# A hybrid transformer trunk: the steps behind each output block are spread over the following blocks

## The chip, the cores and the metric

The kernel runs on one core of a Trainium2 chip. The metric is device time in microseconds, the median of the runs of a kernel; lower is better. The engines are TensorE (PE, with its weight loads shown as PEld), VectorE (DVE), ScalarE (ACT), GpSimd (POOL) and SyncE (SP, whose queue issues nearly all loads). Each takes its own instructions in order and waits for the others by semaphores.

## The reference

The input x is 512 tokens of width 1024 in float32; 16 learned meta tokens are put in front, so 528 rows run through two layers. Each layer adds three things to the running x:

```python
for i in range(DEPTH):
    h = h + 0.5 * swiglu(rmsnorm(h, ffn1_norm[i]), ffn1_w_in[i], ffn1_w_out[i])
    hn = rmsnorm(h, mix_norm[i])
    h = h + (diff_attention(hn, ...) if i % 2 == 0 else gla_mixer(hn, ...))
    h = h + 0.5 * swiglu(rmsnorm(h, ffn2_norm[i]), ffn2_w_in[i], ffn2_w_out[i])
return rmsnorm(h, final_norm)[:, N_META:]
```

SwiGLU is silu(g) * u with [g, u] = h @ w_in (1024 to 2 x 2816), times w_out (2816 to 1024). Attention has 8 heads, each with two softmax maps that are subtracted; GLA (gated linear attention) has 4 heads and goes chunk by chunk.

## The kernel before, in words

Everything is kept transposed: x is eight blocks `xr[0..7]` of 128 features by 528 tokens. The stages run in this order: SwiGLU a, attention (da), SwiGLU b, SwiGLU c, GLA, SwiGLU d. The order of each engine's instructions is written out by hand, so the order of calls in Python is the order of each queue.

Precision: a float32 factor is split in a high part (ACT copies it in a rounded type, fp32r) and a low part (DVE subtracts the high part from it), and a product is three matmuls: high x high, high x low, low x high. Weights come by DMA into the float32 tile `fa` and their parts go into the fp32r tile `ra`.

The input product of a SwiGLU is done by Strassen's scheme on 2 x 2 blocks. For a pair of x blocks (2i, 2i+1) and the two halves of the tokens, x has four quarters: the first (block 2i, first half, `plain` with k = 0, L403), the second and third (block 2i+1, both halves, k = 1), and the fourth (block 2i, second half, `plain2`, L670). Four sums of quarters follow: t1 (L422), t2, t3, t4 (L442, L445, L449), made from `scaled` copies (L415); ACT copies all four (L432), DVE makes their low parts (L435). With the three quarters these are the seven factors kept in `ra` (`seven`); the fourth quarter is kept in the last two hidden slots of the stage, so it is made only at the stage's beginning. It is used by the first hidden blocks alone, which are done plainly (products S1, S3, S2, S4; three blocks in stage a, one in b, c, d); from then on the products are P1, P2, P6, P7, P5, P3, P4. S products hold all four `bank` buffers of PSUM (S1 and S2 share two, S3 and S4 two); P1 of the next block needs one that DVE has read out (L710, or L712 where the root mean square isn't there yet).

The mean square is taken beside all this: `add_square` squares a block on ACT and POOL adds it to `acc` (L343); after the S3 of a stage (in a: after the S4 of block 1) `rms_scale` sums over partitions on PE (L383) and DVE refines the inverse root (L348 to L355).

The weight stream of a SwiGLU (`in_stream`) is a list of tasks: `cut` makes a weight's parts (ACT L597, DVE L622), `add` makes a Strassen sum of weights (DVE L611). After each product so many tasks are done that the parts of six products ahead are ready. After the hidden blocks of the last slab, the stage has a **tail**: eight output blocks j of 24 matmuls. DVE adds the accumulator to `xr[j]` (`out_done`, L849; in attention and GLA `project_out`, L501), which frees one of two accumulators, and then `next_block` makes what the next stage needs of that block:

```python
if kind == "seven":
    plain(i, gcol, tok, k)
add_square(acc, j, c0)
if kind == "seven":
    scaled(i, gcol, tok, k, z)
    if k:
        sums(i, tok, z, last and j == KD - 1)
```

All of a block's steps stand in the queues one behind the other, before the next block's addition. Between them the tail prepares the next stage's first weights (`nxt.to`, `ahead.to`). For stage a there is no tail ahead: `head` makes the quarters from x as it arrives and squares all blocks, and `head_sums` lists twelve steps for the sums, two of which are done behind each of the first products, after the stream's tasks. Until they are through, the stream makes no weight sums (`held`) and the first output weights aren't loaded (`bring`).

In attention, `k_done` (L1078) puts a head's keys in two maps `km` (L1087), in two buffers for alternating heads, which `score` reads (L1137, L1140).

## Time and profile before

| | |
|---|---|
| runs | 2125.42, 2125.94, 2127.83 us; median 2125.94 |
| the profiled execution's own time | 2127.64 us |
| its span, first to last instruction | 2125.9 us |
| busy | PE 1999.4 us (94%), DVE 1677.5 (79%), ACT 1026.2 (48%), POOL 260.5 (12%) |
| mean granted PE clock | 0.967 of 2.4 GHz |
| stages, P1 of b, c, d | at 772.83, 1156.46, 1769.83 us |

The profile is one execution. An engine's busy time is the union of its instructions; idle time is put down to what ended it. The granted clock has two levels, 1.2 and 2.4 GHz (0.5 and 1.0); a value between is a mean over a stretch. Neighbouring instructions of DVE or ACT overlap by about 0.1 us in these rows, so the step from one start to the next is a little shorter than the duration shown.

### The profile page before, as it was taken

The numbers are of one execution on the slowest core, as the hardware profiler recorded it, in microseconds if no ns is written. First come the engines' busy times: TensorE is split into PE (matmuls) and PEld (weight loads), VectorE is DVE, ScalarE is ACT, GpSimd is POOL, SyncE is SP. The second block draws the span as 40 slices with busy tenths as digits, with TensorE's granted clock in tenths as the row PEclk, the third lists the DMA queues.
The fourth block names the chain that finished last, engine by engine and source line by source line (L and its number), as shares of the span: only waits on it lengthen the run. The fifth ranks groups of instructions, "written<-read, shape, count | busy, mean of one in ns | idle before, by whom it ended". The sixth has DMA issues, their size and how long they took to land.

```text
span 2125.9 us, 36706 instructions
## 1 busy us (share of the span) xinstructions
PE 1999.4 (94%) x14672; PEld 1885.6 (89%) x14672; DVE 1677.5 (79%) x3104; ACT 1026.2 (48%) x2055; POOL 260.5 (12%) x193
## 2 busy tenths in 40 slices
PE   6999999999999979999997999999999989999997
PEld 5999999877777879999997999999888868999995
DVE  5888887678887789888867988887565678988884
ACT  6444444445555554444445444444645455544443
POOL 1000000534341200000001000000533310000002
PEclk8999999999998989999998999999999999999998
DMA  4233333111110223333321332332122122333331
GB/s 146 80 105 99 96 100 105 51 50 41 40 49 32 70 75 107 98 104 93 108 75 56 105 102 93 105 100 90 51 70 80 60 89 82 108 99 105 105 100 40
DMA packets 66285, 178.73 MB, mean 84 GB/s; under 512 B 7345, under 2 KB 13618, under 8 KB 66114
## 3 DMA queue, kind: packets, MB, share of 16 engines
q1 hardware_dynamic: 65792, 176.25, 26.6%
q8 instruction: 115, 1.88, 0.3%
q14 instruction: 56, 0.46, 0.1%
q10 hardware_dynamic: 322, 0.13, 0.0%
HBM read 174.26 MB, written 2.10 MB: 83 GB/s over the span
## 4 chain that ended last, share of the span: by engine, by line
PE 72%; DVE 18%; ACT 6%; issue 3%; POOL 1%; DMA 0%; SPq 0%; DVEq 0%; ACTq 0%; POOLq 0%
PE ps_ao L833 6%; PE ps_co L833 6%; PE ps_aA L782 5%; PE ps_cA L782 5%; PE ps_bA L782 5%; PE ps_bo L833 5%; PE ps_do L833 5%; PE ps_dA L782 4%; PE ps_bD L782 3%; PE ps_cD L782 3%; PE ps_aD L782 3%; PE ps_dak L269 2%; DVE ra L622 2%; PE ps_dD L782 2%; PE ps_aB L782 1%
## 5 line engine op out<-in xcount | busy, mean ns | idle before, releaser
L597 ACT CAST ra<-fa 128x512 fp32r<-128x512 f32 x630 | 376.6, 618 | 163.5 <-DVE fa L611 162.7
L622 DVE TENSOR_TENSOR ra<-fa,ra 128x512 fp32r<-128x512 f32 x630 | 426.9, 687 | 14.5 <-ACT ra L597 8.8
L611 DVE TENSOR_TENSOR fa<-fa 128x512 f32<-128x512 f32 x328 | 219.7, 686 | 2.9
L810 DVE TENSOR_TENSOR ra<-fa,ra 128x512 fp32r<-128x512 f32 (+1 forms) x160 | 101.4, 636 | 67.7 <-ACT ra L809 66.9
L225 POOL TENSOR_TENSOR ra<-fa,ra 128x1024 fp32r<-128x1024 f32 x51 | 122.7, 2408 | 158.1 <-ACT ra L222 130.7
L782 PE MATMUL ps_cA<-ra 128*128 128x264 f32 x1008 | 133.5, 284 | 1.8 <-ACT ftc L730 1.2
L782 PE MATMUL ps_bA<-ra 128*128 128x264 f32 x1008 | 133.5, 284 | 1.6 <-ACT ftb L730 1.0
L782 PE MATMUL ps_dA<-ra 128*128 128x256 f32 x1008 | 130.5, 281 | 2.6 <-ACT ftd L730 1.5
L782 PEld LDWEIGHTS ps_dA<-ra 128*128 128x128 f32 x1008 | 126.2, 188 | 7.1 <-ACT ftd L730 2.9
L782 PEld LDWEIGHTS ps_cA<-ra 128*128 128x128 f32 x1008 | 126.7, 188 | 2.8 <-ACT ftc L730 1.6
L782 PEld LDWEIGHTS ps_bA<-ra 128*128 128x128 f32 x1008 | 126.7, 188 | 2.6 <-ACT ftb L730 1.4
L782 PE MATMUL ps_aA<-ra 128*128 128x264 f32 x912 | 122.1, 286 | 3.6 <-DVE fta L710 3.2
L782 PEld LDWEIGHTS ps_aA<-ra 128*128 128x128 f32 x912 | 115.8, 190 | 4.4 <-issue 3.4
L809 ACT CAST ra<-fa 128x512 fp32r<-128x512 f32 (+1 forms) x160 | 91.5, 574 | 0.0
L833 PE MATMUL ps_bo<-hidb,ra 128*128 128x264 f32 x624 | 87.7, 290 | 0.0
L833 PE MATMUL ps_ao<-hida,ra 128*128 128x264 f32 x624 | 84.5, 283 | 0.0
L833 PE MATMUL ps_co<-hidc,ra 128*128 128x264 f32 x624 | 84.5, 283 | 0.0
L833 PEld LDWEIGHTS ps_bo<-hidb,ra 128*128 128x128 f32 x624 | 82.3, 195 | 0.0
L833 PE MATMUL ps_do<-hidd,ra 128*128 128x512 f32 x303 | 79.3, 394 | 0.0
L833 PEld LDWEIGHTS ps_ao<-hida,ra 128*128 128x128 f32 x624 | 79.3, 188 | 0.0
L833 PEld LDWEIGHTS ps_co<-hidc,ra 128*128 128x128 f32 x624 | 79.3, 188 | 0.0
L222 ACT CAST ra<-fa 128x1024 fp32r<-128x1024 f32 x64 | 66.8, 1046 | 5.5 <-issue 2.8
(546 smaller groups left out, 4377.5 us busy)
## 6 DMA issues: line engine op xcount, KB each, us to landing
fa<-in_f_in SPq DMA_DIRECT2D x174, 512.0 KB, 3.6
fa<-in_f_out SPq DMA_DIRECT2D x160, 256.0 KB, 2.7
fa<-in_da_in SPq DMA_DIRECT2D x24, 512.0 KB, 3.5
fa<-in_gla_in SPq DMA_DIRECT2D x24, 512.0 KB, 3.6
fa<-in_f_out SPq DMA_DIRECT2D x32, 128.0 KB, 2.1
fa<-in_da_out SPq DMA_DIRECT2D x8, 512.0 KB, 3.4
fa<-in_gla_out SPq DMA_DIRECT2D x8, 512.0 KB, 3.4
xr<-in_xT SPq DMA_DIRECT2D x8, 264.0 KB, 5.3
```

Source lines behind the costliest of these rows:

```text
L222: act.copy(h, w)
L225: eng.tensor_tensor(out=l, in0=w, in1=h.bitcast(F32), op=ALU.subtract)
L269: nc.tensor.matmul(put(b, at, at + c1 - c0), w[:, ws], x[:, c0:c1], start=first, stop=last,)
L597: act.copy(self.parts(n)[0], self.source(i))
L611: dve.tensor_tensor(out=self.raw(f, x), in0=self.raw(f, a), in1=self.raw(f, b), op=ALU.add)
L622: dve.tensor_tensor(out=l, in0=self.source(i), in1=h.bitcast(F32), op=ALU.subtract)
L782: nc.tensor.matmul(banks[k, f], w[:, ws], v, start=(p in ("P1", "P2", "P7") and i == 0 and c == 0), stop=(i == NQ - 1 and c == 2), skip_gr ...
L809: act.copy(h, raw)
L810: dve.tensor_tensor(out=l, in0=raw, in1=h.bitcast(F32), op=ALU.subtract)
L833: nc.tensor.matmul(ps[:, b, : a1 - a0], w[:, ws], x[:, a0:a1], start=(f == f0 and i == 0), stop=(f == f1 - 1 and i == 2),)
```

## The change

- `next_block` becomes a generator with up to four steps: (1) on ACT: the high parts of the block's quarters, the square, the scaled copy; (2) on DVE: the low parts of the quarters and the block's share of the four sums; for odd blocks also (3) on ACT the copy of the four sums and (4) on DVE their low parts. `follow`, called after a block's addition, takes each waiting generator one step on, does step 1 of the new block, and takes the older ones another step on. `drain` behind the last block finishes the rest. The special finer order for the last block is dropped.
- The fourth quarter is made with the first, for even blocks, in the tail. It lies in a room X2 at the end of `ra` that is shared: hidden slots 6 and 7, the fourth quarters, attention's two pairs of key maps, GLA's q parts and the meta keys' parts use it in turn. The scaled copies of odd pairs' even blocks get a room of their own (`other`).
- The parts of x for attention and GLA (`parts`) are stepped in the same way: the low part comes a block later.
- At the start of a: no squares in `head`; `head_later(u)` is called right behind each of the first nine products, before the stream's tasks, and does two squares (u < 4), the scaled copies of a pair (even u), or its sums and their copy (odd u), and the sums' low part one product later. `held` ends with the ninth product.

```diff
-RA = OB + 2 * L * KD
+X2 = OB + 2 * L * KD
+RA = X2 + NQ * 2 * HALF
...
-NHA = (RA - HB) // (2 * L)
+NHA = (X2 - HB) // (2 * L)
...
+    def second(i):
+        return parts_at(X2 + i * 2 * HALF, HALF)
+    def plain(i, gcol, tok, quarters):
...
+        todo = []
+        for q in quarters:
+            j = 2 * i + (q != 0 and q != 3)
+            x = tokens(xr[j], tok)
+            hl = seven(i)
+            if q == 0:
+                h, l, x = hl[0][:, 0, :n], hl[1][:, 0, :n], x[:, 0]
+            elif q == 1:
+                h, l = hl[0][:, 1:3, :n], hl[1][:, 1:3, :n]
+            else:
+                (h, l), x = [t[:, :n] for t in second(i)], x[:, 1]
+            g = vec[:, gcol + j : gcol + j + 1]
+            act.activation(h, x, AF.Copy, scale=g)
+            todo.append((l, x, g, h))
+        def rest():
+            for l, x, g, h in todo:
+                dve.scalar_tensor_tensor(l, x, g, h.bitcast(F32), op0=ALU.mult, op1=ALU.subtract)
+        return rest
...
-            z[:, 2 * k : 2 * k + 2, :n], tokens(xr[j], tok), AF.Copy,
+            z[k][:, :, :n], tokens(xr[j], tok), AF.Copy,
...
+    def sums(i, tok, z, k):
+        n = SEQ // 2 if tok else HALF
+        (b11, b12), (b21, b22) = [[t[:, c, :n] for c in range(2)] for t in z[:2]]
+        t1, t3, t2, t4 = [z[2][:, c, :n] for c in range(4)]
         if k == 0:
...
+            dve.tensor_tensor(out=t1, in0=b11, in1=b12, op=ALU.subtract)
+            return
+        dve.scalar_tensor_tensor(t2, b22, -1.0, t1, op0=ALU.mult, op1=ALU.subtract)
+        dve.tensor_tensor(out=t3, in0=b22, in1=b12, op=ALU.subtract)
+        dve.scalar_tensor_tensor(t4, t2, -1.0, b21, op0=ALU.mult, op1=ALU.subtract)
+    def cut_sums(i, tok, z, part):
+        n = SEQ // 2 if tok else HALF
+        h, l = [t[:, 3:, :n] for t in seven(i)]
+        if part == 0:
+            act.copy(h, z[2][:, :, :n])
+        else:
+            dve.tensor_tensor(out=l, in0=z[2][:, :, :n], in1=h.bitcast(F32), op=ALU.subtract)
...
+    def room_for_sums(t, other):
+        t, other = [x.rearrange("p (a b) -> p a b", b=HALF) for x in (t, other)]
+        return [[(t[:, 0:2], other)[i % 2], t[:, 2:4], t[:, 4:8]] for i in range(NQ)]
+    def next_block(kind, gcol, acc, j, c0, z=None):
+        if kind == "parts":
+            xh, xl = parts_at(2 * L * j, L)
+            g = vec[:, gcol + j : gcol + j + 1]
+            x = xr[j][:, c0:]
+            act.activation(xh[:, c0:], x, AF.Copy, scale=g)
+            add_square(acc, j, c0)
+            yield
+            dve.scalar_tensor_tensor(
+                xl[:, c0:], x, g, xh[:, c0:].bitcast(F32), op0=ALU.mult, op1=ALU.subtract
             )
-    def sums(i, tok, z, fine):
-        n = SEQ // 2 if tok else HALF
-        h, l = [t[:, :, :n] for t in seven(i)]
-        b12, b21, b22, t1, t3, t2, t4 = [z[:, c, :n] for c in range(1, 8)]
...
-        if fine:
-            out(3, 4)
-        dve.scalar_tensor_tensor(t2, b22, -1.0, t1, op0=ALU.mult, op1=ALU.subtract)
-        if fine:
-            out(5, 6)
-        dve.tensor_tensor(out=t3, in0=b22, in1=b12, op=ALU.subtract)
...
-        else:
-            out(3, 7)
-            rest(3, 7)
...
-            plain(i, gcol, tok, k)
-        add_square(acc, j, c0)
-        if kind == "seven":
-            scaled(i, gcol, tok, k, z)
+            rest = plain(i, gcol, tok, (1,) if k else (0, 3))
+            add_square(acc, j, c0)
+            scaled(i, gcol, tok, k, z[i])
+            yield
+            rest()
+            sums(i, tok, z[i], k)
             if k:
-                sums(i, tok, z, last and j == KD - 1)
-        elif kind is None:
+                yield
+                cut_sums(i, tok, z[i], 0)
+                yield
+                cut_sums(i, tok, z[i], 1)
+        else:
+            add_square(acc, j, c0)
             g = vec[:, V_FIN + j : V_FIN + j + 1]
             act.activation(xr[j][:, c0:], xr[j][:, c0:], AF.Copy, scale=g)
+    pending = []
+    def go_on():
+        for x in list(pending):
+            try:
+                next(x)
+            except StopIteration:
+                pending.remove(x)
+    def follow(gen=None):
+        go_on()
+        before = list(pending)
+        if gen is not None:
+            next(gen, None)
+            pending.append(gen)
+        for x in before:
+            try:
+                next(x)
+            except StopIteration:
+                pending.remove(x)
+    def drain():
+        while pending:
+            go_on()
...
-        z = room_for_sums(fa[:, ZF : ZF + 8 * HALF])
...
-                rest = lambda: next_block("seven", gnext, acc, j, c_next, z, True)
+                rest = lambda: follow(next_block("seven", gnext, acc, j, c_next, z))
...
-            hid = hp.tile([P, (NH - NHA) * 2 * L], F32R, tag="hid", name=f"hid{name}")
...
                     return parts_at(HB + 2 * L * s, L)
+                if s >= NH - 2:
+                    return parts_at(X2 + 2 * L * (s - NH + 2), L)
...
-            second = [
-                [t[:, i * HALF : (i + 1) * HALF] for t in hidden(NH - 2 + k)]
-                for k in range(2) for i in range(2)
-            ]
-            def plain2(i):
-                j = 2 * i
-                g = vec[:, gain + j : gain + j + 1]
-                h, l = [t[:, :n] for t in second[i]]
-                x = tokens(xr[j], tok)[:, 1]
...
             if head:
-                head(z, plain2)
-            else:
-                for i in range(NQ):
-                    plain2(i)
+                head()
...
-                                xh, xl = [t[:, :n] for t in second[i]]
+                                xh, xl = [t[:, :n] for t in second(i)]
...
-                    next_block(kind, gnext, new, j, c0, z, True)
+                    follow(next_block(kind, gnext, new, j, c0, z))
...
-            behind = list(behind()) if behind else []
-            stream.held = bool(behind)
+            stream.held = behind is not None
...
+                if behind and i <= KD:
+                    behind(i)
+                    if i == KD:
+                        stream.held = False
+                        bring(0, 0)
+                        bring(1, 0)
...
                     stream.step()
-                if behind:
-                    for f in behind[:2]:
-                        f()
-                    del behind[:2]
-                    if not behind:
-                        stream.held = False
-                        bring(0, 0)
-                        bring(1, 0)
...
+            drain()
...
-                    km = [bp.tile([P, L], F32R, tag=f"k{m}", name=f"k{m}{h}") for m in range(2)]
+                    assert h < 2 or ("T", h - 2, 0) in kept
+                    c = X2 + h % 2 * 2 * L
+                    km = parts_at(c, L)
...
+            drain()
...
-                kt[nm + "m"] = bp.tile([META, P], F32R, tag=f"ktm{nm}", name=f"ktm{nm}")
+                c = X2 + 2 * SEQ + (nm == "l") * P
+                kt[nm + "m"] = ra[:META, c : c + P]
...
-                    qh = bp.tile([P, SEQ], F32R, tag="qh", name=f"gqh{h}")
-                    ql = bp.tile([P, SEQ], F32R, tag="ql", name=f"gql{h}")
+                    qh, ql = parts_at(X2, SEQ)
...
-                S0 = sp.tile([P, DV], F32, tag="S0", name=f"S0{h}", bufs=1)
+                S0 = fa[:, 3 * CH * P + 7 * L : 3 * CH * P + 7 * L + DV]
...
+            drain()
...
-    def head(z, plain2):
+    z0 = room_for_sums(fa[:, ZF : ZF + 8 * HALF], fa[:, SB : SB + 2 * HALF])
+    def head():
+        lows = []
+        for q, n in ((0, 1), (3, 2)):
+            for i in range(NQ):
+                lows.append(plain(i, V_F1[0], False, (q,)))
+                if q == 0 and i == 0:
+                    first.to(n)
+                lows.pop(0)()
+            if q:
+                first.to(n)
...
-            plain(i, V_F1[0], False, 0)
-            if i == 0:
-                first.to(1)
-        for i in range(NQ):
-            plain2(i)
-        first.to(2)
-        for i in range(NQ):
-            plain(i, V_F1[0], False, 1)
+            plain(i, V_F1[0], False, (1,))()
             if i % 2:
                 first.to(3 + i // 2)
-        for k in (0, 2, 4, 6, 1, 3, 5, 7):
-            add_square(acc, k)
-    def head_sums():
-        zs = room_for_sums(fa[:, ZF : ZF + 8 * HALF])
-        for i in range(NQ):
-            for k in range(2):
-                yield lambda i=i, k=k: scaled(i, V_F1[0], False, k, zs)
-            yield lambda i=i: sums(i, False, zs, False)
...
+    def head_later(u):
+        i, k = divmod(u, 2)
+        if k == 0 and i:
+            cut_sums(i - 1, False, z0[i - 1], 1)
+        if i == NQ:
+            return
+        if u < KD // 2:
+            for j in (u, u + KD // 2):
+                add_square(acc, j)
+        if k == 0:
+            for c in range(2):
+                scaled(i, V_F1[0], False, c, z0[i])
+        else:
+            for c in range(2):
+                sums(i, False, z0[i], c)
+            cut_sums(i, False, z0[i], 0)
     acc = ffn(
         ins["a"], V_F1[0], acc, "a", V_MIX[0], "parts", want_da,
-        aside=[lambda_terms, lambda_spread], head=head, behind=head_sums,
+        aside=[lambda_terms, lambda_spread], head=head, behind=head_later,
```

## Rows read from the trace of the kernel before

**Rows 1.** Six of the waits of PE, whole span: us in total, times, longest

```profile
PE ps_aS L768 <- ACT fa L417: 15.2, 1, 15.2
...
PE ps_dS L768 <- ACT hidd L675: 8.9, 1, 8.9
...
PE ps_bS L768 <- ACT hidb L675: 8.7, 1, 8.7
...
PE ps_cS L768 <- ACT hidc L675: 8.1, 1, 8.1
...
PE ps_bo L833 <- DVE xr L849: 5.5, 2, 3.2
...
PE ps_aA L782 <- DVE fta L710: 3.2, 1, 3.2
```

**Rows 2.** Windows of the start and the three tails: us; busy and count per engine, PEclk, DMA

```profile
24.00:35.40 11.40, 0.01 (x1) 0.04 (x1) 9.02 (x16) 7.95 (x12) 0.81 (x1) 0.51 0.28 92
713.33:751.96 38.63, 33.14 (x264) 31.95 (x262) 30.03 (x40) 22.23 (x33) 8.39 (x6) 0.99 0.25 83
1103.43:1136.62 33.19, 23.01 (x145) 21.86 (x143) 22.33 (x32) 16.00 (x25) 7.93 (x6) 0.80 0.05 16
1711.86:1749.69 37.83, 33.54 (x144) 26.79 (x143) 29.28 (x39) 21.81 (x33) 8.24 (x6) 0.97 0.24 84
```

**Rows 3.** Timeline of b's tail and c's start: start us, us, instruction, idle before

```profile
1103.43 0.70 DVE L849 SCALAR_TENSOR_TENSOR xr<-ps_bo,xr 128x528 f32<-128x528 f32 x1
...
1136.62 0.70 DVE L849 SCALAR_TENSOR_TENSOR xr<-ps_bo,xr 128x528 f32<-128x528 f32 x1
...
1151.33 0.43 DVE L349 TENSOR_SCALAR nA_c<-ps_ss_c 128x264 f32<-128x264 f32 x1 [1.72 <-ACT R_c L348]
...
1156.46 1.62 PE L782 MATMUL ps_cA<-ra 128*128 128x264 f32 x12
```

**Rows 4.** Groups by form, 1103.4 to 1136.6: busy us, mean ns, idle before and releaser

```profile
L435 DVE TENSOR_TENSOR ra<-ftb,ra 128x1056 fp32r<-128x1056 f32 x3 | 3.8, 1259 | 3.5 <-ACT ra L432 3.5
...
L422 DVE TENSOR_TENSOR ftb<-ftb 128x264 f32<-128x264 f32 x4 | 3.7, 928 | 2.7 <-ACT ftb L417 2.7
...
L442 DVE SCALAR_TENSOR_TENSOR ftb<-ftb 128x264 f32<-128x264 f32 x3 | 3.3, 1098 | 1.2 <-ACT ftb L417 1.2
...
L622 DVE TENSOR_TENSOR ra<-fa,ra 128x512 fp32r<-128x512 f32 x4 | 2.7, 682 | 0.0
...
L412 DVE SCALAR_TENSOR_TENSOR ra<-xr,vec,ra 128x528 fp32r<-128x528 f32 x3 | 2.3, 770 | 2.4 <-ACT ra L411 2.4
...
L412 DVE SCALAR_TENSOR_TENSOR ra<-xr,vec,ra 128x264 fp32r<-128x264 f32 x3 | 1.5, 494 | 1.8 <-ACT ra L411 1.8
...
L445 DVE TENSOR_TENSOR ftb<-ftb 128x264 f32<-128x264 f32 x3 | 1.3, 422 | 0.0
...
L343 POOL TENSOR_TENSOR acc_b<-acc_b,sq 128x528 f32<-128x528 f32 x6 | 7.9, 1322 | 372.5 <-ACT sq L339 372.5
```

**Rows 5.** Timeline of stage a's start, as in rows 3

```profile
13.54 0.65 ACT L339 ACTIVATE acc_in<-xr 128x528 f32<-128x528 f32 x1
...
34.82 0.77 DVE L712 COPY fta<-ps_aS 128x264 f32<-128x264 f32 x2
...
66.31 2.98 PE L782 MATMUL ps_aA<-ra 128*128 128x264 f32 x12 [3.22 <-DVE fta L710]
```

**Rows 6.** Timeline of the hand-overs into b and d, as in rows 3

```profile
718.80 1.34 DVE L442 SCALAR_TENSOR_TENSOR fa<-fa 128x264 f32<-128x264 f32 x1 [0.15 <-ACT fa L417]
...
772.83 1.62 PE L782 MATMUL ps_bA<-ra 128*128 128x264 f32 x12
...
1769.83 1.62 PE L782 MATMUL ps_dA<-ra 128*128 128x256 f32 x12
```

**Rows 7.** Timeline in attention, ScalarE's key maps and TensorE's scores, as in rows 3

```profile
464.56 1.29 ACT L1087 CAST k<-k 64x528 fp32r<-64x528 f32 x2 [1.80 <-DVE k L1080]
...
474.25 0.50 PE L1140 MATMUL ps_s<-kl,ra 64*80 64x256 f32 x1
```

More of the change, by code (lines that the diff above doesn't have):

```diff
@@ L398, in tokens @@
         return t[:, L - 2 * n : L].rearrange("p (a b) -> p a b", a=2)
-    def plain(i, gcol, tok, k):
-        j = 2 * i + k
-        g = vec[:, gcol + j : gcol + j + 1]
+    def second(i):
+        return parts_at(X2 + i * 2 * HALF, HALF)
+    def plain(i, gcol, tok, quarters):
         n = SEQ // 2 if tok else HALF
-        x = tokens(xr[j], tok)
-        h, l = seven(i)
-        if k == 0:
-            h, l, x = h[:, 0, :n], l[:, 0, :n], x[:, 0]
-        else:
-            h, l = h[:, 1:3, :n], l[:, 1:3, :n]
-        act.activation(h, x, AF.Copy, scale=g)
-        dve.scalar_tensor_tensor(l, x, g, h.bitcast(F32), op0=ALU.mult, op1=ALU.subtract)
+        todo = []
[16 more added lines that the diff above has]
+        return rest
     def scaled(i, gcol, tok, k, z):
@@ L459, in room_for_sums @@
-    def room_for_sums(t):
-        return t.rearrange("p (a b) -> p a b", b=HALF)
-    def next_block(kind, gcol, acc, j, c0, z=None, last=False):
-        if kind == "parts":
-            split_x(j, gcol, c0)
+            dve.tensor_tensor(out=t1, in0=b11, in1=b12, op=ALU.subtract)
[3 more added lines that the diff above has]
+        dve.scalar_tensor_tensor(t4, t2, -1.0, b21, op0=ALU.mult, op1=ALU.subtract)
@@ L495, in project_out @@
         acc = new_acc(name)
-        z = room_for_sums(fa[:, ZF : ZF + 8 * HALF])
+        z = room_for_sums(fa[:, ZF : ZF + 8 * HALF], fa[:, SB : SB + 2 * HALF])
         def out_block(j):
@@ L648, in ffn @@
         with tc.tile_pool(name=f"h_{name}", bufs=1) as hp:
-            hid = hp.tile([P, (NH - NHA) * 2 * L], F32R, tag="hid", name=f"hid{name}")
+            hid = hp.tile([P, (NH - 2 - NHA) * 2 * L], F32R, tag="hid", name=f"hid{name}")
             ft = hp.tile([P, 8 * HALF], F32, tag="ft", name=f"ft{name}")
-            z = room_for_sums(ft)
+            z = room_for_sums(ft, fa[:, SB : SB + 2 * HALF])
+            gu_ = ft.rearrange("p (a b) -> p a b", b=HALF)
             def hidden(f):
```

25 lines of the change are left out of this document (1 added, 24 removed).

## Prediction

> **What bounds the kernel now.** I read four views in this order. First, whom TensorE (PE) waited for, because PE is busy for 94% of the span and only its idle time can be won: six of the long waits [rows 1] hold 49.6 us, and every one of them stands where a stage begins or hands over to the next. Second, the stretches [rows 2]: in 24.00 to 35.40 PE does nothing while VectorE (DVE) and ScalarE (ACT) work for 9.0 and 8.0 us, and the granted clock is 0.51, that is 1.2 of 2.4 GHz, so work after such a gap starts at half speed. Third, the order of time at one hand-over, from b's tail into c [rows 3]: DVE adds block 1 to x at 1103.43 and block 7 at 1136.62, 33.2 us for six blocks, and stage c's first Strassen product P1 starts at 1156.46. Fourth, DVE's groups in that tail [rows 4]: it waits for ACT (the low part at L412, the sums' low part at L435, the sums at L422 and L442), 11.6 us in all, and while it waits in order, the next block's addition, which alone frees PE's accumulator, stands behind it. DVE's busy time there is 22.3 of 33.19 us; in the tails into b and d it is 30.0 of 38.63 and 29.3 of 37.83 [rows 2]. So the tails are chains of DVE and ACT taking turns, not PE time.
>
> **The three tails into b, c, d.** The change postpones DVE's part of a block to the next block's turn, the copy of its sums one turn on, their low part another. Then DVE finds ACT's operand ready, and its time is its busy time plus what is added. Added: low parts of the fourth quarter, formerly four at the start of the stage (L676), now one per even block; three of them fall before block 7's addition, at 0.41 each (0.49 less the 0.08 by which neighbours overlap [rows 4]): 1.2 us. ACT gets a fourth-quarter copy per even block as well; its busy time in that stretch is 16.0 of 33.19 us [rows 2], so that hides. No DMA, register load or PE instruction is added.
>
> The second price is POOL. It adds each block's square, and a DVE sum that meets this add takes 1.10 instead of 0.42 us (L442 against L445, same shape [rows 4]). Those meetings, four of L422 at 0.51 and three of L442 at 0.68, are already in the busy time, about 0.6 per add. With DVE no longer idle around the add the hold grows: its bounds are 0.6 (as now) and 1.3, the add's own length (1.32 [rows 4]). I take 0.92, because of the row nearest to the new order: in the tail into b a sum right behind other DVE work took 1.34 against 0.42 [rows 6]. That is 0.3 more for each of six adds, 1.9 us per tail. On this the Trainium skill ("SBUF — State Buffer", "SBUF: two separate sides") has a rule that speaks against the change: a DVE instruction with two SBUF inputs and a GpSimd one that reads SBUF exclude each other for the whole instruction. By it each hold would be the add's full length once DVE has no gaps, and the sum 9.6 us smaller, as in the third rival; this trace agrees on the hold (1.10 against 0.42), though it shows mostly a part of one.
>
> Block 1 to block 7 for c: 22.3 + 1.2 + 1.9 = 25.4 instead of 33.2, a gain of 7.8. For b, from block 0 to block 7: 30.0 + 3.1 = 33.1 instead of 38.6, gain 5.5. For d 29.3 + 3.1 = 32.4 instead of 37.8, gain 5.4.
>
> **From block 7 to P1.** DVE's queue in the changed order, for c: block 7's addition 0.62; the sums' low part of blocks 4 and 5, 1.16 (L435); two low parts of block 6, 0.82; its difference 0.34; one hold 0.92; a weight's low part 0.60 (L622); block 7's low part 0.69 and three sums 1.02; a wait for ACT's copy of the sums, 1.17, the one wait that nothing follows to fill (row L435: 3.5 over 3); its low part 1.16; then the stream's own work for the next stage, three weight parts and four weight sums, 4.5 (seven of about L622's size [rows 4]); the wait for ACT's table load and logarithm, which before was 1.72 (L349 [rows 3]) with the squares later than now: between 0 and 1.72, I take 0.9 in the middle; and from L349 to P1 5.1 as now. Together 19.0 us; before, 19.8 (c), 20.9 (b), 20.1 (d), from the additions at 1136.62, 751.96 and 1749.69 (ends of the stretches [rows 2]) to P1 at 1156.46, 772.83 and 1769.83 [rows 3, 6]. Gain 0.8, 1.9, 1.1. The four fourth-quarter pieces themselves thus gain little more: what is late next is **the root mean square's chain on DVE**, with the next stage's weight sums queued ahead of it. PE needs only 13.0 us for the 96 S matmuls ahead of P1 (1.62 for twelve [rows 3]) and some 2 us until block 6's low parts are there: it will be idle for about 4 us before P1, where it had no gap before. Such a gap exists today ahead of stage a's P1 (3.2 us [rows 1]), and the twelve matmuls after it took 2.98 instead of 1.62 us ([rows 5] against [rows 3]). P1 and P2 then lose 2.4, of which 0.6 was idle before P6 anyway: 1.8 us back at each of b, c, d.
>
> Net: c 7.8 + 0.8 - 1.8 = 6.8; b 5.5 + 1.9 - 1.8 = 5.6; d 5.4 + 1.1 - 1.8 = 4.7.
>
> **The start of a.** PE's 15.2 us wait ends at 35.4 [rows 1, 2], when DVE's copies of S2's two banks, from 34.82, free them [rows 5]. They are queued behind sums that are made on a ScalarE which first squares all eight blocks (from 13.54), paced by POOL's adds. Now from 13.54: two squares, two scaled copies and four weight copies on ACT, all of 512 or 528 columns, at 0.54 (the square's 0.65 less the overlap [rows 5]), to 17.9; the last weight's low part 0.6 and four sums at 0.34 on DVE, to 19.9; ACT's copy of the sums 1.08 (twice those columns), DVE's low part 1.16, a weight's low part 0.6 [rows 4], the first bank's copy 0.4: 23.1. Three of POOL's adds fall in between, at 0.92: 25.9. PE resumes 9.5 earlier. The bounds are 0.6 and 1.32 for a hold, 1 us either way, and no gain at all if the sums still come first. The last low part of the sums, formerly before the root mean square, now runs behind it, on the chain to the next wait (P1 of f = 3): 1.2 lost. Holding the weight stream until the ninth product issues two DMAs on SP's queue some units later; their data is wanted three products on, so that costs nothing, and up to one transfer if it doesn't. Net 8.3.
>
> **Edits at nothing.** The pipelined x parts into attention and GLA: those tails already run with PE unbroken, and the waits behind them are for POOL. Moving k, q, the meta keys and S0 into shared room changes no instruction, and keeps as many buffers as before; the bounds are 0 and the second rival.
>
> **Sum.** 8.3 + 5.6 + 6.8 + 4.7 = 25.4. The profiled execution took 2127.64, 1.7 more than its span of 2125.9; less 25.4 that is 2102.2. The median of the runs shown, 2125.94, lies 1.7 below that execution, so I predict **2100**.
>
> **Rivals.**
> 1. *The hand-over is covered wholly*: holds stay at 0.6 (18 tail adds, three at a and three behind block 7 at 0.3: 7 us more), P1 finds its bank free in time (5.4 more): about 38 gained, **2088**; with the start of a down to PE's own pace, 45, 2081. For it: DVE's busy time in c's tail, 22.3, is already near PE's own. Against it: the queue of 19 us behind block 7. Chance 0.22.
> 2. *The shared room makes attention wait* (slower). The place is k_done, where ACT writes the key maps. At 464.56 it writes head 2's, while PE still reads head 1's until 474.75 [rows 7]. If the wait went by the whole room instead of by columns, ACT, and behind it the softmax, would stand for 10 us per head, up to 60 us over six heads; it decides as soon as more than 25.4 of those 60 land on the chain: at half, about **2130**. Against it: other parts of the same large tile are written today beside its readers (L597, L622) with no such wait. Chance 0.06.
> 3. *POOL's adds hold DVE at their full length*, 1.32: 0.4 more than my 0.92 for 24 adds, 9.6 us, so 16 gained: **2110**. For it, the row of 1.34 [rows 6]; against, the mean of L422 [rows 4]. Chance 0.12.
> 4. *It doesn't do what it says*: DVE still meets ACT unfinished because ACT's queue has shifted as well, and the gain at the start is used up behind the root mean square: within 4 us of now, **2125**. Chance 0.05.
>
> **Numbers.** Forecast 0.55, with its own range of 2092 to 2108 from the wait and clock terms. 2081 to 2114 takes in the first rival's lower end and the third with 4 us of ACT waits left; outside lie the slower and the no-change cases and the edges, under 2 in 10. Runs of this kernel spread by 0.11%, so 0.2%, 4.3 us, is about what can be told. Faster 0.55 + 0.22 + 0.12 = 0.89; same 0.05; slower 0.06.
>
> **What would show it.** In the changed profile: PE's waits for L675's fourth quarter gone at b, c, d; DVE's additions in b's tail about 4.2 us apart instead of 5.5, with few waits for ACT; a new PE wait of 3 to 5 us before P1 in b, c, d, released by DVE's bank copy (L710's place), with a clock near 0.5 behind it; PE's wait at the start down to 4 to 6 us; attention's span unchanged. The forecast is wrong if P1 follows its predecessor without a gap (then rival 1), if DVE's sums all take 1.7 (rival 3), or if heads of attention lengthen (rival 2).

## The result, and the profile after

| | before | after |
|---|---|---|
| median | 2125.68 us (4 runs) | 2098.52 us (4 runs, 2095.57 to 2102.78) |
| ratio | | 0.9879, interval 0.985 to 0.9908 |
| the profiled execution, and its span | 2127.64, 2125.9 | 2095.57, 2093.8 |
| busy PE, DVE, ACT | 1999.4, 1677.5, 1026.2 | 1984.3, 1681.0, 1023.1 |
| start to P1 of a | 66.3 | 61.1 |
| block 0's addition to P1 of b, c, d | 59.5, 55.8, 58.0 | 53.7, 46.1, 53.0 |

The kernel became faster by 27.2 us in the median; the forecast was 2100. DVE's busy time is unchanged: the change removed waiting, not work.

First the waits of PE, whole span (us in total, times, longest). They answer to [rows 1]; the line numbers have moved (L768 is L792, L710 is L734, L849 is L873).

```profile
PE ps_aA L806 <- DVE fta L734: 6.9, 1, 6.9
PE ps_aS L792 <- DVE fta L736: 6.8, 2, 4.8
...
PE ps_cS L792 <- DVE ra L425: 5.6, 1, 5.6
PE ps_bS L792 <- DVE ra L425: 4.5, 1, 4.5
PE ps_dS L792 <- DVE ra L425: 4.5, 1, 4.5
PE ps_bA L806 <- DVE ftb L734: 4.0, 1, 4.0
PE ps_cA L806 <- DVE ftc L734: 3.6, 1, 3.6
...
PE ps_dA L806 <- DVE ftd L734: 3.1, 1, 3.1
```

The three waits for the fourth quarter are gone, and 15.2 us at the start have become 6.8 in two parts. In their place stand a wait for block 6's low parts (L425, 4.5 to 5.6 us) and one ahead of each P1 (3.1 to 4.0 us, where there was none), and P1 of a waits 6.9 instead of 3.2.

The windows of the three tails, from the first to the last addition, with the same columns as [rows 2]:

```profile
702.00:736.31 34.31, 31.91 (x262) 31.48 (x260) 28.25 (x41) 23.43 (x37) 8.88 (x6) 1.00 0.29 93
1085.66:1110.93 25.27, 19.33 (x154) 18.55 (x152) 19.95 (x34) 18.09 (x31) 8.42 (x6) 0.99 0.07 21
1682.94:1716.63 33.69, 31.50 (x142) 25.73 (x140) 27.68 (x39) 23.09 (x37) 8.35 (x6) 1.00 0.29 94
```

The tail from b into c takes 25.27 us for blocks 1 to 7 instead of 33.19. DVE's busy time in it is 19.95, though, not the whole stretch. Where the other 5.3 us are is seen in the order of time of that tail and of c's start (start us, us, instruction, idle before it and what ended it); it answers to [rows 3]:

```profile
1085.66 0.71 DVE L873 SCALAR_TENSOR_TENSOR xr<-ps_bo,xr 128x528 f32<-128x528 f32 x1 [0.74 <-PE ps_bo L857]
...
1093.58 1.97 DVE L425 SCALAR_TENSOR_TENSOR ra<-xr,vec,ra 128x264 fp32r<-128x264 f32 x2
...
1100.75 0.69 DVE L662 TENSOR_TENSOR ra<-fa,ra 128x512 fp32r<-128x512 f32 x1 [1.93 <-ACT ra L637]
...
1103.14 1.99 DVE L425 SCALAR_TENSOR_TENSOR ra<-xr,vec,ra 128x264 fp32r<-128x264 f32 x2
...
1108.32 1.30 POOL L344 TENSOR_TENSOR acc_b<-acc_b,sq 128x528 f32<-128x528 f32 x1 [3.49 <-ACT sq L340]
...
1110.32 0.69 DVE L662 TENSOR_TENSOR ra<-fa,ra 128x512 fp32r<-128x512 f32 x1 [1.92 <-ACT ra L637]
1110.93 0.70 DVE L873 SCALAR_TENSOR_TENSOR xr<-ps_bo,xr 128x528 f32<-128x528 f32 x1
...
1112.71 1.97 DVE L425 SCALAR_TENSOR_TENSOR ra<-xr,vec,ra 128x264 fp32r<-128x264 f32 x2
...
1113.25 6.77 PE L792 MATMUL ps_cS<-ra 128*128 128x264 f32 x38 [5.57 <-DVE ra L425]
...
1130.33 2.36 PE L806 MATMUL ps_cA<-ra 128*128 128x264 f32 x12 [3.56 <-DVE ftc L734]
```

Two low parts of the weight stream (L662) wait 1.93 and 1.92 us for ScalarE's copy of the same weight: that copy stands in ACT's queue behind all of the block's own steps. Three L425 pairs take 1.97 to 1.99 us, where pairs that meet no add of POOL's take 0.89: the add holds them up (such a delay is called a hold below). POOL's add at 1108.32, on the other hand, falls into DVE's wait and holds nothing. Block 6's low parts (1112.71) stand behind the second wait, block 7's addition and the sums' low part; PE waits for them until 1113.25.

The start of a, which answers to [rows 5]:

```profile
18.86 1.57 DVE L446 SCALAR_TENSOR_TENSOR fa<-fa 128x264 f32<-128x264 f32 x1
...
25.71 4.45 PE L792 MATMUL ps_aS<-ra 128*128 128x264 f32 x24 [4.79 <-DVE fta L736]
...
26.79 1.37 DVE L446 SCALAR_TENSOR_TENSOR fa<-fa 128x264 f32<-128x264 f32 x1
28.08 1.55 DVE L447 TENSOR_TENSOR fa<-fa 128x264 f32<-128x264 f32 x1
...
32.18 9.00 PE L792 MATMUL ps_aS<-ra 128*128 128x264 f32 x72 [2.02 <-DVE fta L736]
...
61.13 2.98 PE L806 MATMUL ps_aA<-ra 128*128 128x264 f32 x12 [6.88 <-DVE fta L734]
```

PE goes on at 25.71, but the sums of the next pair are held as well (1.37 and 1.55 us where such a sum alone takes 0.43), and PE stops again for 2.0 us at 32.18.

### The profile page after: what moved, and what is told of

Same layout as the page of the kernel before. It is cut to its first block, busy times and chain, and to the rows that moved or that the text cites. A ratio compares the mean times of both kernels' runs of the same rounds, so it can differ in the third digit from the quotient of the medians.

```text
span 2093.8 us, 36697 instructions
## 1 busy us (share of the span) xinstructions
PE 1984.3 (95%) x14672; PEld 1875.5 (90%) x14672; DVE 1681.0 (80%) x3095; ACT 1023.1 (49%) x2046; POOL 263.6 (13%) x193
## 4 chain that ended last, share of the span: by engine, by line
PE 72%; DVE 18%; ACT 6%; issue 3%; POOL 0%; DMA 0%; SPq 0%; DVEq 0%; ACTq 0%; POOLq 0%
PE ps_ao L857 6%; PE ps_co L857 6%; PE ps_bA L806 6%; PE ps_bo L857 5%; PE ps_cA L806 5%; PE ps_aA L806 5%; PE ps_do L857 5%; PE ps_dA L806 4%; PE ps_bD L806 3%; PE ps_cD L806 3%; PE ps_aD L806 3%; PE ps_dak L270 2%; PE ps_dD L806 2%; DVE ra L662 2%; PE ps_bB L806 1%
## 5 line engine op out<-in xcount | busy, mean ns | idle before, releaser
L662 DVE TENSOR_TENSOR ra<-fa,ra 128x512 fp32r<-128x512 f32 x630 | 425.5, 685 | 22.2 <-ACT ra L637 16.4
L857 PE MATMUL ps_bo<-ra 128*128 128x264 f32 x624 | 86.0, 284 | 2.7 <-DVE xr L873 1.8
L857 PE MATMUL ps_co<-ra 128*128 128x264 f32 x624 | 85.8, 284 | 0.8 <-ACT ra L833 0.7
L857 PE MATMUL ps_ao<-ra 128*128 128x264 f32 x624 | 85.7, 283 | 0.9 <-DVE ra L834 0.9
L857 PE MATMUL ps_do<-ra 128*128 128x512 f32 x309 | 82.1, 395 | 0.9 <-ACT ra L833 0.7
L857 PEld LDWEIGHTS ps_bo<-ra 128*128 128x128 f32 x624 | 79.7, 188 | 3.5 <-issue 2.2
L857 PEld LDWEIGHTS ps_co<-ra 128*128 128x128 f32 x624 | 79.7, 188 | 1.3 <-ACT ra L833 0.9
L857 PEld LDWEIGHTS ps_ao<-ra 128*128 128x128 f32 x624 | 79.7, 188 | 1.1 <-DVE ra L834 1.1
```

Of the source, the lines that this page charges most:

```text
L662: dve.tensor_tensor(out=l, in0=self.source(i), in1=h.bitcast(F32), op=ALU.subtract)
L857: nc.tensor.matmul(ps[:, b, : a1 - a0], w[:, ws], x[:, a0:a1], start=(f == f0 and i == 0), stop=(f == f1 - 1 and i == 2),)
```

## The experiments

All of them edit the changed kernel. Its own time is 2094.1 us (run e5_after_again, beside e6 to e8; e1 to e4 ran in an earlier group), and the kernel before took 2121.9 to 2122.5 in the four groups of runs, so differences below are against 2094.1. The 95% intervals of the ratios reach 0.0012 to 0.0021 (2.5 to 4.5 us) to either side. Where two runs differ by some 5 us or less, what an edit did is therefore read from the traces, and the medians alone hardly show it. Times from one mark to another (P1, block 0's addition) are those of the profiled executions.

**e1: the steps of a block issued at once**

```diff
     def follow(gen=None):
-        go_on()
-        before = list(pending)
...
+        for _ in gen:
+            pass
```

> The fourth quarter stays in the tails and the new start of stage a stays, but all steps of a block are issued at once behind its addition, as before the change. Theory (the pipeline carries the gain of the tails, 5.8 + 7.0 + 4.8 us between the last additions of the profile of after and those of before): DVE meets ACT unfinished again, block 1 to block 7 of b's tail into c takes 33 us or more instead of 25.3, and the time is some 2098.5 + 16 = 2114 us. Rival (the fourth quarter's removal from the stage's start carries it): block 1 to block 7 is slow too, but it is made up in the hand-over, and the time is 2099 to 2103 us.

Measured: 2117.75 us (12 runs), ratio 0.9986 (0.9971 to 1.0001): 23.7 us slower (16 were expected), nearly all of the change undone. DVE's waits between block 1 and block 7 of b's tail (us in total, times, longest):

```profile
DVE ra L425 <- ACT ra L420: 4.2, 6, 0.8
DVE ra L456 <- ACT ra L454: 3.4, 3, 1.1
```

The waits for ACT that the prediction read in [rows 4] are back, at the same places, and blocks 1 to 7 take 34.3 us (1093.23 to 1127.51). In its three tails, block 0 to P1, this run loses 4.5, 9.4 and 4.7 us against e5 and stands 1.3, 0.3 and 0.2 us below the kernel before. So the pipeline carries the gain of the tails; the fourth quarter made in the tail without it is worth hardly anything.

**e2: the start of a as before**

```diff
-    def head_later(u):
...
+    def head_sums():
+        for i in range(NQ):
+            for k in range(2):
+                yield lambda i=i, k=k: first_sums(i, k)
+            yield lambda i=i: last_sums(i)
```

> Only the start of stage a is as before: all squares ahead of the first products, the sums in twelve steps behind the stream's tasks. Theory (the profile of after: P1 of a at 61.1 instead of 66.3): 5 us longer, 2103.5 us, with PE's wait of 15.2 us for the second S2 product back. Rival (my forecast of 8.3 us was right and the profile's 5.2 us is a chance of that execution): 2107 us. Second rival (what is gained at the start is lost again in the products behind it, as DVE has the same work): 2098.5 us.

Measured: 2099.36 us, ratio 0.9905 (0.9886 to 0.9923), 5.3 us slower. TensorE's timeline at the start:

```profile
35.34 14.17 PE L792 MATMUL ps_aS<-ra 128*128 128x264 f32 x96 [15.50 <-ACT fa L434]
...
65.83 1.72 PE L806 MATMUL ps_aA<-ra 128*128 128x264 f32 x12 [3.25 <-DVE fta L734]
```

The wait of 15.5 us is back and P1 of a comes at 65.83, 4.9 us later than in e5. The theory held in the trace: the new start is worth 5 us up to P1, not the 8.3 of the forecast. The medians' intervals don't tell 5 from 8. Behind P1 the old start gets 1.6 us back here (stage a from P1 to the next root mean square takes 331.6 us, in e5 333.2), as its P1 ran at the full clock (last section).

**e3: the fourth quarter at the stage's start**

```diff
-            rest = plain(i, gcol, tok, (1,) if k else (0, 3))
+            rest = plain(i, gcol, tok, (1,) if k else (0,))
...
             if head:
                 head()
+            else:
+                for i in range(NQ):
+                    plain(i, gain, tok, (3,))()
```

> The pipeline stays, but the fourth quarter is made at the beginning of b, c and d, as before the change. Theory (the end of a hand-over is set by DVE's chain through the root mean square, in which the four low parts stand either way; three of them move from ahead of block 7's addition to behind it): PE waits 3 to 6 us longer for S3 in each stage, but P1 comes only 1 to 2 us later, and the time is 2101 to 2104 us. Rival (the fourth quarter's place carries the gain, the 8.1 to 8.9 us waits of before come back in full): 2098.5 + 18 to 24 = 2117 to 2122 us.

Measured: 2103.45 us, ratio 0.9923 (0.9905 to 0.9941), 9.4 us slower. The time itself lies in the theory's 2101 to 2104, but that was counted from 2098.5; as a loss, 9.4 lies between the theory's 2.5 to 5.5 and the rival's 18 to 24. TensorE at c's start:

```profile
1121.88 0.81 PE L795 MATMUL ps_cS<-ra 128*128 128x264 f32 x2 [4.42 <-DVE ra L425]
1127.17 0.59 PE L795 MATMUL ps_cS<-ra 128*128 128x264 f32 x1 [4.48 <-ACT ra L420]
...
1141.84 1.62 PE L809 MATMUL ps_cA<-ra 128*128 128x264 f32 x12
```

S now waits twice, 4.42 and 4.48 us, and P1 follows without a gap: here TensorE's own S products set P1, 22.3 us after block 7 instead of 19.4. My theory that the root mean square's chain sets P1 either way fell for this order. Block 0 to P1 is 2.9, 4.9 and 0.3 us longer than in e5 (b, c, d). In c 2.0 of the 4.9 come before block 7: with the low parts gone, five sums instead of two pairs meet POOL's adds (1.56 to 1.57 us each), which the theory left out. The products behind P1 follow without a gap and give 3.3 us back, so that the stages show 4.8 of the 9.4; attention and GLA took 10 us longer in this execution. The two parts of the change depend on each other: the pipeline makes the tail short, and the quarter's place keeps part of that, most of it in c and hardly any in d.

**e4: no adds on GpSimd in the tails** (an edit of `add_square` in `next_block`; what is left out stands in the expectation)

> Left out: GpSimd's adding up of the squares in the tails into b, c and d (21 adds), so the mean square holds block 0 alone. Theory (a DVE sum that meets such an add is held some 1.0 us): block 1 to block 7 of the tail into c falls from 25.3 to about 21 us, the chain from block 7 to P1 by 1 us, b's and d's tails by 2 to 3 us each and their chains by 1: 12 us in all, 2086 us. Rival (the hold costs 0.3 us or hides behind PE's own pace and the waits for ACT): 2094 to 2098 us.

Measured: 2089.34 us, 4.8 us faster, where 12 were expected. In the profile the three tails, block 0 to P1, are 4.5, 2.8 and 3.4 us shorter than in e5; attention and GLA ran 3.0 us longer each in that execution. DVE in b's tail:

```profile
1097.21 0.89 DVE L425 SCALAR_TENSOR_TENSOR ra<-xr,vec,ra 128x264 fp32r<-128x264 f32 x2
...
1098.60 0.69 DVE L662 TENSOR_TENSOR ra<-fa,ra 128x512 fp32r<-128x512 f32 x1 [0.16 <-ACT ra L637]
...
1103.54 0.69 DVE L662 TENSOR_TENSOR ra<-fa,ra 128x512 fp32r<-128x512 f32 x1 [1.92 <-ACT ra L637]
```

The L425 pair takes 0.89, so the hold is what the adds cost. But blocks 1 to 7 still take 23.3 us: the L662 ahead of block 7 waits 1.92 as before, and the one ahead of block 6 now waits 0.16 too. Once the holds are gone, ScalarE's weight copy is the next limit.

**e5: the changed kernel again**

> The changed kernel itself, unedited, as the measure for the three runs beside it on the same chip. It should stand to the kernel before as it did, 0.988. Theory on its profile (attention and GLA differ between executions by the granted clock alone): the tails and the start repeat within 1 us, the main parts of attention and GLA differ by several us. Rival: they repeat too, and the shared room is what shortened them.

Measured: 2094.09 us, ratio 0.9876 (0.986 to 0.9893). Blocks 1 to 7 of b's tail take 25.27 us as in the first profile, and block 7 to P1 agrees within 0.1 us in all three stages; the main part of attention takes 304.8 instead of 307.9.

**e6: block 6's low parts at once**

```diff
             scaled(i, gcol, tok, k, z[i])
-            yield
+            if j != KD - 2:
+                yield
             rest()
```

With this edit block 6's first sum is also made ahead of the copy of the previous pair's sums, out of the same room, so that one of those sums is overwritten, here and in the next two runs; the copy then waits for it, and block 7's addition comes 2 us later, at each hand-over.

> Block 6's low parts (the last even block) are made right behind its own ScalarE step, not one block later. Theory (two chains end at P1: TensorE's S products, and the root mean square, for which ScalarE first makes weight copies that wait for VectorE's weight sums): PE's wait of 4.5 to 5.6 us in S goes down to 1 or 2, the wait ahead of P1 grows by nearly as much, and P1 comes 0 to 1.5 us earlier per stage: 0 to 5 us less than the unedited kernel. Rival (the S products alone set P1): 3 to 4 us per stage, some 10 us less.

Measured: 2100.11 us, 6.0 slower. TensorE at c's start:

```profile
1110.82 6.29 PE L793 MATMUL ps_cS<-ra 128*128 128x264 f32 x38 [1.18 <-DVE ra L425]
1118.35 1.16 PE L384 MATMUL ps_ss_c<-acc_b,ones 128*128 128x264 f32 x4 [1.24 <-POOL acc_b L344]
...
1133.54 2.76 PE L807 MATMUL ps_cA<-ra 128*128 128x264 f32 x11 [8.20 <-DVE ftc L735]
```

The wait in S went from 5.57 to 1.18 us, as expected, plus 1.24 for POOL's last add; the wait ahead of P1 grew from 3.56 to 8.20. TensorE was ready 4.6 us sooner, and P1 still comes 18.7 us after block 7, against 19.4. The S products don't set P1 in the changed kernel; VectorE's queue does.

**e7: and the root mean square first**

```diff
+                first3 = not head and i < 3
+                if first3:
+                    n_steps = 0 if i else 3
                 for _ in range(n_steps):
                     stream.step()
...
+                    if first3 and i == 2:
+                        while stream.done < goal:
+                            stream.step()
```

> As the run before, and in b, c and d the last weight sum, the weight copies and low parts that stood between S1 and S2 in the queues are made behind S2's evacuation, so that the root mean square goes first. Theory: ScalarE's logarithm follows the sum of squares by 2 us instead of 4, and P1 comes 4 to 6 us earlier per stage: 12 to 18 us less than the unedited kernel. Rival (the weight sums that are put off are late for P6): half of that comes back as a wait at P6, 6 us less.

Measured: 2105.11 us, 5.0 slower than e6. VectorE's first step of the root mean square, then TensorE's P1 and P6 of c:

```profile
1126.62 0.42 DVE L350 TENSOR_SCALAR nA_c<-ps_ss_c 128x264 f32<-128x264 f32 x1
...
1131.07 2.32 PE L807 MATMUL ps_cA<-ra 128*128 128x264 f32 x12 [2.39 <-DVE ftc L735]
...
1138.48 2.84 PE L807 MATMUL ps_cA<-ra 128*128 128x264 f32 x12 [2.72 <-ACT ftc L748]
```

L350 no longer waits, and P1 comes 14.4 us after block 7 instead of 18.7. But P6 then waits 2.72 us, because its accumulator is read behind the weight sums that were put off, and c, from P1 to the next root mean square, takes 358.5 us instead of 354.3: 4.1 of the 4.3 us gained are given back, and in b and d 3.4 of 4.3 and 3.8 of 4.5. The rival held, with nearly the whole of it instead of half (GLA's main part, 203.2 us here and 198.6 in e6, is most of what the two runs differ by). Reordering VectorE's queue in the hand-over wins next to nothing, since the queue is full from block 6 to P6; only less work, fewer holds or fewer waits on it can.

**e8: and copies early, and two adds fewer** (the edits are those of e9's first hunk and e10)

> As the run before, and two more: in b's tail the stream's weight copy is issued on ScalarE ahead of a block's steps, and the squares of blocks 6 and 7 are summed by TensorE (four more matmuls of 0.39 us per stage) instead of GpSimd's last two adds. Theory (each of the two 1.9 us waits of VectorE for ScalarE, and each 1.0 us hold, stands on the chain to P1): 3 to 4 us less at c and 1 to 2 at each of b, c, d, 6 to 9 us less than the run before. Rival (with the root first, TensorE goes at its own pace through the hand-over and nothing on VectorE counts): the same time as the run before.

Measured: 2093.45 us, 11.7 us less than e7, more than the 6 to 9 expected, yet no better than the unedited kernel. Against e5, block 0 to P1 is 5.4, 8.1 and 5.6 us shorter (b, c, d), but the stages behind P1 are 5.8, 3.8 and 3.6 us longer, as in e7, and attention and GLA took 10.5 us longer in this execution. Blocks 1 to 7 of b's tail: 23.0 instead of 27.2 us.

**e9: weight copies ahead of the block's steps**

```diff
+                if kind == "seven" and j >= 3:
+                    nxt.hi(nxt.done)
                 out_done(tail, j)
...
+                for n in {6: (2, 3), 7: (4,)}.get(j, ()):
+                    ahead.hi(n)
                 run(b)
```

> The changed kernel with one reordering of ScalarE's queue: the next stage's weight copies in the three tails (one per block from block 3 in b's, those of blocks 6 and 7 in attention's and GLA's) are issued ahead of the block's own steps. Nothing is added or left out. Theory (after the change each tail is set by a loop of VectorE and ScalarE: VectorE's weight low part waits 1.9 us for the copy, twice in b's tail, once in the other two, and the next addition stands behind it): block 1 to block 7 in b's tail 25.3 minus 3.8 = 21.5 us, P1 of c 3 to 4 us earlier, of b and d 1.5 to 2 each, 6 to 8 us in all, a ratio of 0.984 to the kernel before. Rival (VectorE finds the block's other copies late instead): 0 to 2 us, ratio 0.987.

Measured: 2125.89 us, 31.8 slower. The second hunk did what I had not seen: in attention's and GLA's tails the room of these weight parts still holds the output weights of blocks 6 and 7. The last of those are copied at 722.92 (ScalarE, in attention's tail), the early copies follow from 727.67 and overwrite part of them, so that the products of these two blocks wait for the copies and multiply by wrong parts (in this run and the next). TensorE's waits, whole span, have a new line (GLA's product has another, of 12.3 us):

```profile
PE ps_dao L270 <- ACT ra L637: 12.9, 2, 8.5
```

Block 0 to P1 is 15.1 us longer in b and 14.2 in d than in e5. That is the price of a shared room in which an order is broken. The first hunk, in b's tail, can be read alone. VectorE there, the additions of blocks 1 and 7 and the low part ahead of the second:

```profile
1101.26 0.71 DVE L873 SCALAR_TENSOR_TENSOR xr<-ps_bo,xr 128x528 f32<-128x528 f32 x1 [0.74 <-PE ps_bo L857]
...
1119.59 0.68 DVE L662 TENSOR_TENSOR ra<-fa,ra 128x512 fp32r<-128x512 f32 x1
...
1123.12 0.69 DVE L873 SCALAR_TENSOR_TENSOR xr<-ps_bo,xr 128x528 f32<-128x528 f32 x1
```

No L662 waits any more, and blocks 1 to 7 take 21.86 us instead of 25.27; 21.5 was expected.

**e10: and the last two squares summed on TensorE**

```diff
-            add_square(acc, j, c0)
+            add_square(acc, j, c0, add=j < KD - 2)
...
+            terms = [acc] + extra
+            for m, t in enumerate(terms):
```

> As the run before, and the squares of blocks 6 and 7 are summed by TensorE, in four more matmuls per stage, instead of by GpSimd's last two adds. Theory (each of these two adds holds VectorE for 1.0 us on the chain to P1; with the copies early nothing else takes the hold's place): 2 us less per stage, 5 to 6 less than the run before. Rival (as without the adds altogether, where the time fell by 5 us instead of 12, a wait for ScalarE takes the hold's place): 1 to 2 us less.

Measured: 2120.97 us, 4.9 less than e9. Block 7 to P1 falls from 19.3, 19.8 and 19.3 us (b, c, d) to 18.2, 18.5 and 18.2: 1.1 to 1.3 us, about one hold per stage, where the theory had two. The time agrees with the theory; of the 4.9 us the three chains show 3.5.

**e11: no adds at the start**

> The changed kernel; left out are GpSimd's seven adds of the squares at the start of stage a alone, so that its mean square holds block 0 only. Theory (my forecast for the start, 8.3 us, fell short by 3 because five sums on VectorE were held 1.1 us each by these adds, and everything up to P1 of a is one VectorE queue): P1 of a at 56 instead of 61, and the time 4 to 5 us less than the unedited kernel. Rival (P1 of a is set by the weight sums held back until the ninth product, whatever stands ahead of them): P1 of a 0 to 2 us earlier.

Measured: 2092.11 us, ratio 0.9872 (0.9851 to 0.9893), 2 us faster than e5, which the intervals don't tell apart. In the profile P1 of a comes 5.8 us earlier than in e5, and stage a behind it takes 333.2 us in both; attention took 308.6 us here and 304.8 in e5. VectorE's first full sum, and P1:

```profile
18.78 0.43 DVE L446 SCALAR_TENSOR_TENSOR fa<-fa 128x264 f32<-128x264 f32 x1
...
55.18 2.98 PE L806 MATMUL ps_aA<-ra 128*128 128x264 f32 x12 [6.80 <-DVE fta L734]
```

The sum takes 0.43 instead of 1.57, and P1 of a comes at 55.18. Its wait is 6.8 (6.9 in the first profile, 5.3 in e5): all of VectorE's queue up to P1 has moved. So the holds of the start's adds cost 5.8 us up to P1, and it is not the weight sums held back that set P1.

**e12: what is left, without the order broken** (e9's first hunk, e10, and `add=u < KD // 2 - 1` in `head_later`; nothing is left out)

> The changed kernel with three edits that leave nothing out: in b's tail alone the next stage's weight copies are issued ahead of the block's steps; in the three tails the squares of blocks 6 and 7, and at the start of a those of blocks 3 and 7, are summed by TensorE instead of by GpSimd's last two adds. Theory (VectorE's queue sets every hand-over, so only waits and holds on it that are removed count): from block 0 to P1 of c 41.8 us instead of 46.1 as in the run before with both edits, b and d 1 to 2 us each, P1 of a 2 us earlier: 8 to 10 us less than the unedited kernel, a ratio of 0.983 to 0.984 to the kernel before. Rival (what P1 gains is given back behind it, where VectorE has the same weight sums to make, as in the run with the root first): ratio 0.986 to 0.988.

Measured: 2085.11 us (5 runs), ratio 0.9837 (0.9819 to 0.9854): 9.0 us faster than the changed kernel and 37 faster than the one before. P1 of a, b, c and d and, around block 1 and 7, VectorE in b's tail:

```profile
58.65 2.98 PE L814 MATMUL ps_aA<-ra 128*128 128x264 f32 x12 [5.20 <-DVE fta L742]
...
750.76 1.71 PE L814 MATMUL ps_bA<-ra 128*128 128x264 f32 x12 [1.07 <-DVE ftb L742]
...
1080.09 0.71 DVE L881 SCALAR_TENSOR_TENSOR xr<-ps_bo,xr 128x528 f32<-128x528 f32 x1 [0.74 <-PE ps_bo L865]
...
1101.95 0.70 DVE L881 SCALAR_TENSOR_TENSOR xr<-ps_bo,xr 128x528 f32<-128x528 f32 x1
...
1120.46 1.73 PE L814 MATMUL ps_cA<-ra 128*128 128x264 f32 x12
...
1724.90 1.66 PE L814 MATMUL ps_dA<-ra 128*128 128x256 f32 x12 [0.58 <-DVE ftd L742]
```

P1 of a comes 2.3 us earlier than in e5; block 0 to P1 is 1.1 (b), 4.3 (c) and 1.0 us (d) shorter: 8.6 in all, close to the 9.0 of the medians. The waits ahead of P1 of b and d are down to 1.07 and 0.58 us, c's is gone, and the products of b and d take 1.71 and 1.66 us where the changed kernel's took 2.98 and 2.90. So the four stages behind P1 are another 3.8 us shorter together; attention and GLA took 2.6 us longer in this execution.

## Why the prediction was right, point by point

**Block 1 to block 7.** Forecast 25.4 for c, measured 25.27; 33.1 for b, measured 34.31; 32.4 for d, measured 33.69. The totals hold, their make-up doesn't. "DVE finds ACT's operand ready, and its time is its busy time plus what is added" was wrong for one operand that I had not listed, the weight stream's copy: of the 5.3 us in which DVE is idle there, 3.8 are waits for it (L662), 1.2 for PE and 0.2 for the sums' copy. On the other side the holds came out at 2.5 us instead of 6 x 0.92: two of c's six adds within the stretch hold VectorE by 1.1 us each, one by 0.3, and the others fall where it waits. And the sums' low part of blocks 4 and 5, 1.2 us, had been counted twice, here and behind block 7. These errors nearly cancel, and that is luck. e1 shows that the pipeline itself is what the time hangs on, e4 and e9 that holds and copies are the two next limits. The forecast also left out block 0's own steps: its addition and block 1's stood 2.8 us apart in c (1100.63 and 1103.43) and now 1.4 (1084.22 and 1085.66).

**The hold.** The Trainium skill ("SBUF — State Buffer", "SBUF: two separate sides") says that a VectorE instruction with two SBUF inputs and a GpSimd one that reads SBUF exclude each other for the whole instruction. The trace agrees: 1.97 against 0.89 us for the pair, 1.57 against 0.43 for a sum, and both fall to the lower value without the adds (e4, e11). The copies that read PSUM weren't held: the two L736 at 25.14 take 0.76 us amid POOL's adds, as long as L712's before the change [rows 5]. A hold ends with the add, so its length depends on where in the add it begins: before, an add from 1105.58 to 1106.91 met a sum that started at 1106.10 and ended at 1107.19, so 0.67 us were lost; after, the second L425 of a pair starts 0.3 us or less behind the add and loses 1.1. The rival that applied the rule to all 24 adds, 2110, still fell, as not every add meets such work.

**From block 7 to P1.** Forecast 19.0, measured 19.4 in all three stages; e6 and e7 show that VectorE's queue sets it, as forecast, in the order that the change made. The "some 2 us until block 6's low parts are there" were 2.3 in all three (c: from 1110.93 to 1113.25); the whole wait of 4.5 to 5.6 us begins before block 7's addition, because the low parts stand behind the copy's wait. It didn't count, since P1 hung on the other chain (e6). The forecast gap of about 4 us ahead of P1 was 4.0, 3.6 and 3.1.

**The clock.** I charged 1.8 us per stage for a cold P1 and P2. From P1's start to the fourth product before the change 5.2 us passed, and now 5.9 (b), 6.0 (c) and 7.0 (d): 0.7, 0.8 and 1.8. The granted clock in P1's twelve products was 0.50 in b and d and 0.67 in c.

**The start of a** is the term that was mis-sized: forecast 8.3, measured 5.2 in the profiles and 5.3 by e2's median. PE resumed at 25.71 (forecast 25.9). The failing step was the sum's holds: "Three of POOL's adds fall in between" charged them for the first pair only, and the second pair's stood at nothing. Four more adds, from 24.5 to 30.8, hold the second pair's sums, PE stops again, and the whole queue up to P1 is late. e11 prices it: from the first bank's copy to the one that frees P1 VectorE took 30.9 us before, 35.4 after and 31.8 without the adds. So the second pair's holds are 3.6 us, and the "1.2 lost" was 0.9. With the first pair's 2.3, all holds of the start come to 6.0 against the first profile (5.8 against e5).

**Sum.** From these readings: a 5.2; b 5.8 - 0.7; c 8.4 + 1.4 (block 0's steps) - 0.8; d 4.9 - 1.8: 22.3 of the 25.4 forecast. The two profiled executions differ by 32.1, the medians by 27.2. The rest stands in the main parts of attention and GLA, 6.4 and 4.0 us (0.6 is lost again behind the fourth products of a and c). Their work is the same before and after, and whether the change has a share in those 10.4 us is open (below). So a forecast within 2 us of the median had its terms 3.1 too high and this luck in its favour.

**Rivals.** The hand-over wholly covered: not in this change, but e12 comes to 2085 with what this rival asked for, smaller holds and P1 hardly waiting. Attention slowed by the shared room: PE's wait for VectorE's `sm` in its scores is 14.2 us before and after, and ScalarE's key maps wait for VectorE's `k` alone, 16.8 us before and 16.7 after, so no; e9 shows that such a room can cost, where an order is broken. No effect: no.

## What to carry to other kernels

When a pipeline removes the waits of an in-order queue, list every operand that this queue takes from the other engine, also those of unrelated work between the steps: the first one left out becomes the new limit. Behind a full queue, moving an instruction forward only moves the wait (e6, e7); taking a wait or a hold off it is worth most of its length (e9: 3.4 of 3.8 us in b's tail; e12), as long as no other wait takes its place (e4). A slow engine's instruction that locks the fast one costs nothing where the fast one waits anyway, so price it by its place and not by its count.

## What the runs showed of the hardware

**The granted clock differs between executions in parts that are the same.** The main parts of attention and of GLA (us; busy and count of PE, PEld, DVE, ACT, POOL; PEclk, DMA share, GB/s), first in the profile before:

```profile
399.00:713.33 314.33, 287.95 (x1834) 245.22 (x1835) 250.89 (x645) 155.92 (x406) 108.28 (x91) 0.93 0.14 44
1509.20:1711.86 202.66, 195.73 (x1189) 166.86 (x1190) 122.98 (x213) 104.10 (x205) 71.80 (x37) 0.97 0.21 68
```

And in e5:

```profile
394.10:698.94 304.84, 277.44 (x1834) 236.85 (x1835) 252.54 (x645) 156.03 (x406) 108.22 (x91) 0.97 0.15 45
1481.20:1679.85 198.65, 191.33 (x1189) 163.53 (x1190) 123.39 (x213) 103.88 (x205) 71.72 (x37) 1.00 0.23 69
```

Instruction counts and the busy time of VectorE and ScalarE agree within 1%; TensorE's clock is 0.93 and 0.97 in the one and 0.97 and 1.00 in the other, and 13.5 us go with it. The changed kernel's own two profiles have 307.9 and 304.8 us in attention at 0.96 and 0.97. Among the changed kernel's variants attention takes 304.8 to 312.8 us and GLA 198.6 to 203.9, so one profile can't say whether the change has a share in this; that the medians of e1 and e5 differ by 5 us more than their tails leaves it open. How much of these 10 to 14 us is the change's own is not shown.

**A gap of the same length has two outcomes.** P1 of a follows a gap of 3.22 us in the profile before and of 3.25 in e2: its twelve matmuls took 2.98 us there [rows 5], at a granted clock of 0.50, and 1.72 here, at 1.00. A price for a cold start can therefore only be given as a range.
